# Gate column sums, late sums and output scaling placed elsewhere in a hybrid trunk layer

## The chip, the cores and the metric

One Trainium2 chip; the kernel runs on one core. The time is the device time of one launch in microseconds (us), of which three runs give the median. The engines are TensorE (PE; its weight loads are PEld), VectorE (DVE), ScalarE (ACT), GpSimd (POOL) and SyncE (SP); transfers between HBM and the on-chip memory are started from the queues of SP and POOL.

## What is computed

One layer of a decoder trunk in float32, with 512 positions, width 2048, and two branches that are merged by gates:

```python
mod = c_act @ w_ada[l] + b_ada[l]
shift, scale, gate = jnp.split(mod, 3, axis=-1)
h = rms_norm(x, g_pre[l]) * (1.0 + scale[:, None, :]) + shift[:, None, :]
p = h @ w_in[l]
cv, cg, cz, q, k, v, az, m_conv, m_attn = jnp.split(p, offsets, axis=-1)
y_conv = conv_branch(cv, cg, cz, ...)        # GLU, causal depthwise conv, layer norm, silu, silu(cz), projection
y_attn = attn_branch(q, k, v, az, ...)       # differential attention, rms norm, silu(az), projection
merged = jax.nn.sigmoid(m_conv) * y_conv + jax.nn.sigmoid(m_attn) * y_attn
out = merged @ w_o[l]
x = x + gate[:, None, :] * rms_norm(out, g_post[l])
```

The vector `gate` is the last third of `mod`: 2048 column sums of `c_act` times a 2048 x 2048 part of `w_ada`.

## The kernel before

**Matmuls.** A float32 product is emulated: `split` writes a value as a high part (a cast on ACT, line 145) and a low part (a subtraction on DVE, line 146), and `mm3` (line 167) makes three matmuls of them. So every weight tile that PE uses, `wh_...` and `wl_...`, comes through ACT and then DVE. Weights are fetched by SP (`wr_...`, up to 1 MB each, three buffers).

**Stages.** After the front, the first projections and the attention heads (0 to about 600 us) come, in this order: the last groups of the az projection (`gemm2`, tiles `pg_az`), three stages of `gemm_blocks` called cz (4 blocks), ma (8) and mc (8), the two branch projections ya and yc (`gemm_y`, tiles `py_ya`, `py_yc`, eight groups each), and the output projection by `w_o` in two column halves G=0 and G=1 (`oprod`, tiles `oz`, `or`, `ox`, `oy`). `gemm_blocks` makes a 2x2 block product with seven products z, x, y instead of eight; each needs a weight operand that is a sum of blocks (`ws_...`, DVE), split again. The output projection does the same, and for it the merged activations get block sums (`mt1`, `mt23`, `mt4`) while yc runs.

**Background work.** A deque `work` holds Python generators. `pump(n)` takes n steps from the first one, and is called between groups of matmuls: after each product of `gemm_blocks` (`rate[0]`, 1 there), after each group of ya (YP = 3) and of yc (3). `pump()` without a number runs all that is left. The block sums of `h` for cz (`block_sums`) are such a generator, and so is `gate(n)`, n = 0 to 3, for 512 columns of `gate` each: 16 steps, in each of which POOL starts the load of a 256 KB tile `adag` two steps ahead and DVE adds one tile times a scalar to `accg` (line 668); then one matmul with a matrix of ones, `pgt`, sums over the partitions and hands the result to every row; then `bg` and `gg` (lines 673 and 674). gate(1) is the first of the work in the az stage, gate(0) runs in mc stretched by `spread` to one step for every three products, gate(2) in ya, gate(3) in yc.

**Order.** The instructions of an engine run in the order that the tile scheduler gives them, which follows the program order, the dependencies and the free buffers; `paced` and `ordered` pin chains of them. A waiting instruction holds up all that stands behind it on its engine.

**End of yc, and the output.** The groups of yc go j = 0, 4, 1, 5, 2, 6, 3, 7; for each DVE merges two tiles `ga` (fetched by SP, lines 959 and 960), and for j >= 4 makes `mt23` and `mt4` (lines 972 to 974). Their splits are put into a list `late` and done during the first products of G=0 (`late_splits`). In G=1 the last `a22`, `a12` operands are prepared ahead (`held`), the rows of blocks 2 and 3 are scaled by `rstd` on ACT and added to x by accumulating DMAs of POOL (`xr2`, line 1209), and stored by SP (line 1212); blocks 0 and 1 follow (`finish`, line 1072).

## Time and profile before

| what | us |
|---|---|
| median of 3 runs | 1445.31 |
| lowest and highest | 1442.08, 1445.92 |
| the profiled execution, whole run | 1444.37 |
| its span (first to last instruction) | 1442.6 |
| PE busy in the span | 1383.1 |
| DVE busy in the span | 1159.9 |
| ACT busy in the span | 561.7 |

Times in the rows below count from the start of the span. The profiled execution is 1.8 us longer than its span. "Busy" is the time in which an engine worked on at least one instruction; for each instruction group the views give what ended the idle time before it. PEclk is the granted TensorE clock as a share of full speed.

### The profile page before, as it was taken

What the parts mean: (1) busy time and instruction counts of PE and PEld (TensorE: products, weight loads), DVE (VectorE), ACT (ScalarE), POOL (GpSimd) and SP (SyncE); (2) the same over time, 40 slices, a digit from 0 to 9 for tenths busy, and PEclk for the clock granted to TensorE, in tenths of its full rate; (3) what the DMA queues carried; (4) which work ended last, traced back from release to release, by engine and by line L of the source; (5) the groups of instructions that cost most, each with busy time, mean ns of one, the idle gap of its engine ahead of it and who ended that gap; (6) DMA issues with size and microseconds to landing.
All of it is one profiled execution on the core that took longest, in us unless ns stands there. A gap on an engine that the chain in (4) does not pass through costs nothing.

```text
span 1442.6 us, 20701 instructions
## 1 busy us (share of the span) xinstructions
PE 1383.1 (96%) x7903; PEld 1173.2 (81%) x7903; DVE 1159.9 (80%) x1882; ACT 561.7 (39%) x907; POOL 59.8 (4%) x103
## 2 busy tenths in 40 slices
...
GB/s 310 280 276 304 235 121 117 117 102 67 109 67 95 102 67 109 197 111 131 197 154 188 177 169 190 232 157 164 135 217 347 290 146 190 204 117 199 177 236 263
DMA packets 178758, 254.90 MB, mean 177 GB/s; under 512 B 10065, under 2 KB 120994, under 8 KB 178274
## 3 DMA queue, kind: packets, MB, share of 16 engines
...
## 4 chain that ended last, share of the span: by engine, by line
PE 78%; DVE 12%; DMA 5%; issue 3%; ACT 2%; SPq 0%; DVEq 0%; POOL 0%; ACTq 0%; POOLq 0%
PE pc L167 10%; PE py_ya L167 6%; PE pv L167 6%; PE pg_k L167 6%; PE pg_q L167 5%; PE x_ma L167 4%; PE x_mc L167 4%; PE pg_az L167 4%; PE y_mc L167 3%; PE y_ma L167 3%; PE z_ma L167 3%; PE z_mc L167 3%; PE x_cz L167 3%; PE oy L167 2%; PE or L167 2%
## 5 line engine op out<-in xcount | busy, mean ns | idle before, releaser
L500 DVE SCALAR_TENSOR_TENSOR cacc<-u,cw,cacc 128x511 f32<-128x511 f32 (+14 forms) x240 | 164.5, 729 | 0.0
L167 PE MATMUL pc<-hp,wh_c 128*128 128x512 f32 x512 | 159.8, 397 | 3.3 <-DVE part L369 1.2
L167 PEld LDWEIGHTS pc<-hp,wh_c 128*128 128x128 f32 x512 | 95.4, 189 | 29.3 <-issue 2.7
L167 PE MATMUL pc<-hp,wl_c 128*128 128x512 f32 x256 | 98.7, 395 | 2.1 <-DVE wl_c L146 2.1
L369 DVE TENSOR_TENSOR part<-pc,part 128x512 f32<-128x512 f32 x96 | 64.7, 688 | 25.4 <-PE pc L167 24.9
L167 PE MATMUL pv<-wh_v,hp 128*128 128x512 f32 x256 | 82.8, 397 | 0.9 <-DVE part L369 0.9
L167 PE MATMUL pg_q<-hp,wh_q 128*128 128x512 f32 x256 | 82.7, 399 | 0.0
L167 PE MATMUL pg_az<-hp,wh_az 128*128 128x512 f32 x256 | 82.1, 400 | 0.0
L167 PE MATMUL pg_k<-hp,wh_k 128*128 128x512 f32 x256 | 80.1, 392 | 0.0
L167 PE MATMUL py_ya<-ya,wh_ya 128*128 128x512 f32 x256 | 78.9, 389 | 0.0
L145 ACT CAST wh_c<-wr_c 128x1024 fp32r<-128x1024 f32 (+1 forms) x36 | 34.2, 956 | 104.6 <-PE pc L167 46.1
L167 PEld LDWEIGHTS pc<-hp,wl_c 128*128 128x128 f32 x256 | 48.4, 190 | 14.1 <-DVE wl_c L146 3.3
L167 PEld LDWEIGHTS pv<-wh_v,hp 128*128 128x128 f32 x256 | 47.8, 188 | 14.3 <-issue 4.5
L167 PEld LDWEIGHTS pg_az<-hp,wh_az 128*128 128x128 f32 x256 | 48.6, 191 | 12.3 <-issue 2.7
L652 POOL DMA_DIRECT2D adag<-in_w_ada_dram x64 | 34.4, 538 | 560.5 <-ACT ta_ma L753 277.8
L167 PEld LDWEIGHTS pg_q<-hp,wh_q 128*128 128x128 f32 x256 | 47.2, 188 | 12.4 <-issue 2.8
L167 PEld LDWEIGHTS py_ya<-ya,wh_ya 128*128 128x128 f32 x256 | 48.0, 188 | 9.9
L167 PEld LDWEIGHTS pg_k<-hp,wh_k 128*128 128x128 f32 x256 | 47.9, 188 | 9.4
L167 PE MATMUL pg_az<-hp,wl_az 128*128 128x512 f32 x128 | 50.8, 402 | 2.4 <-DVE wl_az L146 2.4
L167 PE MATMUL py_yc<-ych,wh_yc 128*128 128x512 f32 x128 | 50.8, 397 | 1.2 <-DVE ga L959 1.2
L307 DVE SCALAR_TENSOR_TENSOR acc<-ada,cact,acc 128x512 f32<-128x512 f32 (+1 forms) x52 | 50.5, 971 | 1.1 <-DMA ada<-in_w_ada_dram 0.9
L167 PE MATMUL py_yc<-ycl,wh_yc 128*128 128x512 f32 x128 | 51.1, 399 | 0.0
...
## 6 DMA issues: line engine op xcount, KB each, us to landing
ada<-in_w_ada_dram SPq DMA_DIRECT2D x128, 256.0 KB, 5.4
...
```

The lines of the kernel that those rows point to most:

```text
L145: nc.scalar.copy(hi, src)
L167: mm = nc.tensor.matmul(ps, a[p], b[q], start=start and i == 0, stop=stop and i == 2, skip_group_check=more)
L307: nc.vector.scalar_tensor_tensor(acc, raw[:, kk - k0, :, :], cact[:, kk:kk + 1], acc, op0=ALU.mult, op1=ALU.add)
L369: nc.vector.tensor_tensor(part[i], ps[f], part[i], op=ALU.add)
L500: paced(nc.vector.scalar_tensor_tensor(cvo[t][:, s:], u[t][:, :S - s], wj, cvo[t][:, s:], op0=ALU.mult, op1=ALU.add))
L652: nc.gpsimd.dma_start(out=raws[k], in_=ada_v[:, k, 2 * D + n * 512:2 * D + (n + 1) * 512])
```

## The change

It moves work and leaves the arithmetic as it was: gate(1) runs in mc behind gate(0) and `spread` is gone; each gate yields LAG = 5 more times ahead of its `pgt`; yc pumps four steps per group instead of three; in the last group of yc (j = 7) the sums `mt23`, `mt4` are put into `late` as well, and `late_steps` does four of its entries after the first products and two after each of the next; the last sum of G=0, `q + oy`, is placed inside the first step of G=1; in the tail the scaling and adding of row block 2 (`join(0)`) is placed between the preparation of the third and the fourth weight group.

```diff
@@ -667,6 +667,8 @@
             else:
                 nc.vector.scalar_tensor_tensor(acc, raws[k], s1, acc, op0=ALU.mult, op1=ALU.add)
             yield
+        for _ in range(LAG):
+            yield
         pgt = bank("t", 1, f"pgt_{n}")
         nc.tensor.matmul(pgt, ones, acc, start=True, stop=True)
         yield
@@ -678,13 +680,6 @@
             gg[0] = gp
         yield
 
-    def spread(steps, n):
-
-        for _ in steps:
-            for _ in range(n):
-                yield
-
-    work.append(gate(1))
     for pair in range(4):
         if pair == 1:
             work.append(block_sums())
@@ -851,7 +846,7 @@
             spill(f"cz{2 * pair + f}", gs[f])
     for c0, name in ((C_MA, "ma"), (C_MC, "mc")):
         if name == "mc":
-            work.append(spread(gate(0), 3))
+            work.extend((gate(0), gate(1)))
         for j in range(8):
             z, ta, tb = gemm_blocks(w_in[0], c0 + j * 256, f"{name}{j}")
             g0, g1 = temp(f"{name}0_{j}"), temp(f"{name}1_{j}")
@@ -933,10 +928,13 @@
     mB, mT1, mT23, mT4, late = [None] * KT, [None] * KH, [None] * KH, [None] * KH, []
     b12, t1 = {}, {}
 
-    def late_splits(n):
-        for _, g, hi, lo in late[:n]:
-            split(g, hi(), lo())
-        del late[:n]
+    def late_steps(n):
+        for _, step in sorted(late, key=lambda e: e[0])[:n]:
+            step()
+        late[:] = sorted(late, key=lambda e: e[0])[n:]
+
+    def late_split(order, g, hi, lo):
+        late.append((order, lambda: split(g, hi(), lo())))
 
     def late_page(box, i, name):
         def get():
@@ -968,22 +966,29 @@
                 split(u1, hi[:, H2:], lo[:, H2:])
                 continue
             split(g, hi, lo)
-            t23 = temp(f"mt23_{kk}")
-            nc.vector.tensor_tensor(t23[:, :H2], g[:, H2:], t1[j - 4][:, half], op=ALU.add)
-            nc.vector.tensor_tensor(t23[:, H2:], b12[kk][:, H2:], g[:, H2:], op=ALU.subtract)
-            nc.vector.tensor_tensor(t4[:, half], g[:, :H2], t23[:, :H2], op=ALU.subtract)
-            if kk < 4:
-                hi, lo = mT23[kk] = page(f"mt23h_{kk}", F32R), page(f"mt23l_{kk}", F32R)
-                split(t23, hi, lo)
+
+            def sums(kk=kk, half=half, g=g, u1=t1[j - 4][:, half], t4=t4, now=j < 7):
+                t23 = temp(f"mt23_{kk}")
+                nc.vector.tensor_tensor(t23[:, :H2], g[:, H2:], u1, op=ALU.add)
+                nc.vector.tensor_tensor(t23[:, H2:], b12[kk][:, H2:], g[:, H2:], op=ALU.subtract)
+                nc.vector.tensor_tensor(t4[:, half], g[:, :H2], t23[:, :H2], op=ALU.subtract)
+                if kk < 4:
+                    hi, lo = mT23[kk] = page(f"mt23h_{kk}", F32R), page(f"mt23l_{kk}", F32R)
+                    split(t23, hi, lo)
+                else:
+                    mT23[kk] = [None, None]
+                    late_split(kk if now else 8 + kk, t23, late_page(mT23[kk], 0, f"mt23h_{kk}"),
+                               late_page(mT23[kk], 1, f"mt23l_{kk}"))
+
+            if j < 7:
+                sums()
             else:
-                mT23[kk] = [None, None]
-                late.append((0, t23, late_page(mT23[kk], 0, f"mt23h_{kk}"), late_page(mT23[kk], 1, f"mt23l_{kk}")))
+                late.append((kk, sums))
         if j >= 4:
             mT4[j - 4] = [None, None]
-            late.append((1, t4, late_page(mT4[j - 4], 0, f"mt4h_{j}"), late_page(mT4[j - 4], 1, f"mt4l_{j}")))
-        pump(3)
+            late_split(16 + j, t4, late_page(mT4[j - 4], 0, f"mt4h_{j}"), late_page(mT4[j - 4], 1, f"mt4l_{j}"))
+        pump(4)
     pump()
-    late.sort(key=lambda e: e[0])
 
 
     fss = small(16, "fss")
@@ -1128,12 +1133,16 @@
                 p1()
                 paced(nc.vector.tensor_tensor(s1, a21, s1, op=ALU.add))
                 p7()
+                if G and t == 0:
+                    for i in range(2):
+                        nc.vector.tensor_tensor(u2[i], oy[i], u2[i], op=ALU.add)
+                        out_later(0, 2 + i, u2[i], u2[i], temp(f"osq12_0_{i}"))
                 p6()
                 p5()
             if t == 0:
                 out_now()
             if G == 0:
-                late_splits(2)
+                late_steps((4, 2, 2, 2)[t])
         if G:
 
             og01 = [pair_of(f"og01_{i}", F32) for i in range(2)]
@@ -1161,9 +1170,7 @@
                         nc.vector.tensor_tensor(g, orr[i], q[i], op=ALU.subtract)
                         out_later(1, i, g, g, temp(f"osq21_{G}_{i}"))
                 oprod(oy, wop_of(s2[2 * t:2 * t + 2], f"os4_{G}_{t}"), oB22, t, False)
-            for i in range(2):
-                nc.vector.tensor_tensor(q[i], oy[i], q[i], op=ALU.add)
-                out_later(0, 2 + i, q[i], q[i], temp(f"osq12_{G}_{i}"))
+            u2 = q
             continue
 
         oprod(oz, w12, oB21, 0, False)
@@ -1181,32 +1188,40 @@
                 og[t][n] = page(f"ogf_{n}_{t}")
                 fetch(f"og_{n}_{t}", og[t][n])
         held = []
-        for t in range(4):
+
+        def columns(t):
             rb = wraw(w_o[0], KH + 2 * t, 2, c0, 1024, f"ob_{G}_{t}") if t else rb0
-            a12, a22 = rb[:, :, :S], rb[:, :, S:]
-            if t < 2:
-                oprod(orr, wop(a22, f"oa22_{G}_{t}"), oT4, t, False)
-                if t:
-                    oprod(oz, wop(a12, f"oa12_{G}_{t}"), oB21, t, False)
-            else:
-                held.append((t, [wop_of([a[:, k, :] for k in range(2)], f"{n}_{t}", t == 2)
-                                 for a, n in ((a22, "oa22"), (a12, "oa12"))]))
-            if t == 1:
-                for i in range(2):
-                    g = temp(f"oc12_{i}")
-                    nc.vector.tensor_tensor(g, oy[i], q[i], op=ALU.add)
-                    out_done(2, 2 + i, g, og23[i][:, 0, :], page(f"osq12_{G}_{i}"))
-                sums3(2, 2)
-                r = rstd(2, 2)
+            return rb[:, :, :S], rb[:, :, S:]
+
+        def hold(t):
+            a12, a22 = columns(t)
+            held.append((t, [wop_of([a[:, k, :] for k in range(2)], f"{n}_{t}", t == 2)
+                             for a, n in ((a22, "oa22"), (a12, "oa12"))]))
+
+        def join(i):
+            for a, g in enumerate((og01[i], og23[i])):
+                nc.scalar.mul(g, g, r[:, i:i + 1])
+                nc.gpsimd.dma_start(out=xr2[i][a], in_=g, accum_op=ALU.add)
+
+        oprod(orr, wop(columns(0)[1], f"oa22_{G}_0"), oT4, 0, False)
+        a12, a22 = columns(1)
+        oprod(orr, wop(a22, f"oa22_{G}_1"), oT4, 1, False)
+        oprod(oz, wop(a12, f"oa12_{G}_1"), oB21, 1, False)
+        for i in range(2):
+            g = temp(f"oc12_{i}")
+            nc.vector.tensor_tensor(g, oy[i], q[i], op=ALU.add)
+            out_done(2, 2 + i, g, og23[i][:, 0, :], page(f"osq12_{G}_{i}"))
+        sums3(2, 2)
+        r = rstd(2, 2)
+        hold(2)
+        join(0)
+        hold(3)
+        join(1)
         xrs = []
         for i in range(2):
             xr = wp.tile([P, 4, 512], F32, tag="wr", name=f"xr_{i}")
             nc.sync.dma_start(out=xr.rearrange("p k n -> p (k n)"), in_=x2[i * P:(i + 1) * P, :])
             xrs.append(xr)
-        for i in range(2):
-            for a, g in enumerate((og01[i], og23[i])):
-                nc.scalar.mul(g, g, r[:, i:i + 1])
-                nc.gpsimd.dma_start(out=xr2[i][a], in_=g, accum_op=ALU.add)
         for i in range(2):
             for a in range(2):
                 nc.sync.dma_start(out=out2[(2 + i) * P:(3 + i) * P, a * 1024:(a + 1) * 1024],
```

How the scheduler's order changes, on DVE. First the az stage: the rows up to the split `wl_az2_0`, on which the third of the four az groups (`pg_az2`) waits. Names end in running numbers; `accg_1` and `adag_1_k` are gate(1), `hf`, `t1`, `t4`, `t23l` the block sums of `h`, `sz` the silu of an az group. Before:

```order
L668 SCALAR_TENSOR_TENSOR accg_1_5000<-adag_1_12_5089,cact_111,accg_1_5000 128x512
L621 TENSOR_TENSOR hf1_0_5241<-hp_0_341 128x512
L668 SCALAR_TENSOR_TENSOR accg_1_5000<-adag_1_13_5092,cact_111,accg_1_5000 128x512
L621 TENSOR_TENSOR hf2_0_5242<-hp_8_1387 128x512
L668 SCALAR_TENSOR_TENSOR accg_1_5000<-adag_1_14_5137,cact_111,accg_1_5000 128x512
L627 TENSOR_TENSOR t1_0_4942<-hf1_0_5241 128x256
L668 SCALAR_TENSOR_TENSOR accg_1_5000<-adag_1_15_5144,cact_111,accg_1_5000 128x512
L628 TENSOR_TENSOR hf1_0_5241<-hf1_0_5241,hf2_0_5242 128x256
L702 SCALAR_TENSOR_TENSOR sz_2_5272<-sz_2_5272,pg_az1_0_5129 128x512
L702 SCALAR_TENSOR_TENSOR sz_3_5277<-sz_3_5277,pg_az1_1_5130 128x512
L673 TENSOR_TENSOR bg_1_5139<-pgt_1_5177,bg_1_5139 128x512
L146 TENSOR_TENSOR wl_az2_0_5287<-wr_az2_0_5284,wh_az2_0_5286 128x1024
```

In the changed kernel:

```order
L621 TENSOR_TENSOR hf1_1_5167<-hp_1_515 128x512
L621 TENSOR_TENSOR hf2_1_5168<-hp_9_1392 128x512
L627 TENSOR_TENSOR t1_0_4942<-hf1_1_5167 128x256
L628 TENSOR_TENSOR hf1_1_5167<-hf1_1_5167,hf2_1_5168 128x256
L146 TENSOR_TENSOR wl_az1_12_5198<-wr_az1_8_5155,wh_az1_12_5197 128x1024
L630 TENSOR_TENSOR hf1_1_5167<-hf2_1_5168,t1_0_4942 128x256
L631 TENSOR_TENSOR t4_0_5128<-hf2_1_5168,hf1_1_5167 128x256
L146 TENSOR_TENSOR t23l_1_5204<-hf1_1_5167,t23h_1_5203 128x512
L146 TENSOR_TENSOR t4l_1_5208<-t4_0_5128,t4h_1_5207 128x512
L621 TENSOR_TENSOR hf1_2_5211<-hp_2_723 128x512
L621 TENSOR_TENSOR hf2_2_5212<-hp_10_1397 128x512
L146 TENSOR_TENSOR wl_az2_0_5255<-wr_az2_0_5252,wh_az2_0_5254 128x1024
```

The column sums and `bg_1` are gone from this stage; the block sums stand there now, further on by one `k` and a half than before when the same split comes. In mc, gate(0) and gate(1) stand with one `accg` per product.

Second the yc stage, around the last two column sums of gate(3) and the tiles `ga_4` and `ga_5` of the group j = 2. Before:

```order
L146 TENSOR_TENSOR wl_yc3_4_11780<-wr_yc3_11749,wh_yc3_4_11779 128x1024
L146 TENSOR_TENSOR mgs_4_11630<-mt1_2_11625,mgs_4_11630 128x256
L959 SCALAR_TENSOR_TENSOR ga_5_11636<-ga_5_11636,py_yc2_1_11566 128x512
L668 SCALAR_TENSOR_TENSOR accg_3_11265<-adag_3_14_11646,cact_111,accg_3_11265 128x512
L960 TENSOR_TENSOR ga_5_11636<-mg_4_10719,ga_5_11636 128x512
L966 TENSOR_TENSOR mt1_2_11625<-ga_5_11636 128x256
L668 SCALAR_TENSOR_TENSOR accg_3_11265<-adag_3_15_11653,cact_111,accg_3_11265 128x512
L146 TENSOR_TENSOR mgs_5_11640<-ga_5_11636,mgs_5_11640 128x256
```

In the changed kernel:

```order
L146 TENSOR_TENSOR wl_yc3_0_11752<-wr_yc3_11749,wh_yc3_0_11751 128x1024
L668 SCALAR_TENSOR_TENSOR accg_3_11265<-adag_3_14_11565,cact_111,accg_3_11265 128x512
L668 SCALAR_TENSOR_TENSOR accg_3_11265<-adag_3_15_11572,cact_111,accg_3_11265 128x512
L957 SCALAR_TENSOR_TENSOR ga_4_11638<-ga_4_11638,py_yc2_0_11577 128x512
L958 TENSOR_TENSOR ga_4_11638<-mg_4_10719,ga_4_11638 128x512
L964 TENSOR_TENSOR mt1_2_11637<-ga_4_11638 128x256
L146 TENSOR_TENSOR wl_yc3_4_11780<-wr_yc3_11749,wh_yc3_4_11779 128x1024
L146 TENSOR_TENSOR mgs_4_11642<-ga_4_11638,mgs_4_11642 128x256
L146 TENSOR_TENSOR mgs_4_11642<-mt1_2_11637,mgs_4_11642 128x256
L957 SCALAR_TENSOR_TENSOR ga_5_11648<-ga_5_11648,py_yc2_1_11578 128x512
```

`accg` 14 and 15 stood behind `ga_5` and stand ahead of `ga_4` now. On SP's queue the loads `wr_yc3` and `wr_yc7` stand ahead of two `ga` fetches each (`ga_2`, `ga_3` and `ga_10`, `ga_11`), which were ahead of them, and two fetches of `gg` ahead of `ga_4`.

Third the end of yc, up to the splits `wl_os2` for the first `ox` products of the output projection. Before:

```order
L146 TENSOR_TENSOR mt23l_6_12092<-mt23_6_11896,mt23h_6_12091 128x512
L959 SCALAR_TENSOR_TENSOR ga_15_11900<-ga_15_11900,py_yc7_1_11829 128x512
L960 TENSOR_TENSOR ga_15_11900<-mg_14_11104,ga_15_11900 128x512
L972 TENSOR_TENSOR mt23_7_11907<-ga_15_11900,mt1_3_11807 128x256
L973 TENSOR_TENSOR mt23_7_11907<-ga_7_11818,ga_15_11900 128x256
L146 TENSOR_TENSOR mgs_15_11904<-ga_15_11900,mgs_15_11904 128x512
L974 TENSOR_TENSOR mt4_7_11888<-ga_15_11900,mt23_7_11907 128x256
L1104 TENSOR_TENSOR os2_0_0_11981<-os1_0_0_11929,wr_oa_0_0_11927 128x512
L1104 TENSOR_TENSOR os2_0_1_11983<-os1_0_0_11929,wr_oa_0_0_11927 128x512
L146 TENSOR_TENSOR mt23l_7_12096<-mt23_7_11907,mt23h_7_12095 128x512
L146 TENSOR_TENSOR wl_os2_0_0_11986<-os2_0_0_11981,wh_os2_0_0_11985 128x512
L146 TENSOR_TENSOR wl_os2_0_0_11986<-os2_0_1_11983,wh_os2_0_0_11985 128x512
```

In the changed kernel:

```order
L146 TENSOR_TENSOR mgs_14_11893<-ga_14_11889,mgs_14_11893 128x512
L958 TENSOR_TENSOR ga_15_11896<-mg_14_11104,ga_15_11896 128x512
L146 TENSOR_TENSOR wl_os3_0_0_11958<-wr_oa_0_0_11919,wh_os3_0_0_11957 128x1024
L146 TENSOR_TENSOR mgs_15_11900<-ga_15_11896,mgs_15_11900 128x512
L1109 TENSOR_TENSOR os2_0_0_11973<-os1_0_0_11921,wr_oa_0_0_11919 128x512
L1109 TENSOR_TENSOR os2_0_1_11975<-os1_0_0_11921,wr_oa_0_0_11919 128x512
L972 TENSOR_TENSOR mt23_6_12005<-ga_14_11889,mt1_3_11807 128x256
L146 TENSOR_TENSOR wl_os2_0_0_11978<-os2_0_0_11973,wh_os2_0_0_11977 128x512
L973 TENSOR_TENSOR mt23_6_12005<-ga_6_11808,ga_14_11889 128x256
L974 TENSOR_TENSOR mt4_7_11888<-ga_14_11889,mt23_6_12005 128x256
L972 TENSOR_TENSOR mt23_7_12009<-ga_15_11896,mt1_3_11807 128x256
L146 TENSOR_TENSOR wl_os2_0_0_11978<-os2_0_1_11975,wh_os2_0_0_11977 128x512
```

Most sums of the last group (`mt23`, `mt4`) stood ahead of the sums `os2` and the splits `wl_os2`; all but one of those ahead of the first split stand behind it now, as do `mt23l_6` and `mt23l_7`.

## Rows read from the trace of the kernel before

**Rows 1.** The page, busy us, share of the span, instructions.
```profile
PE 1383.1 (96%) x7903; PEld 1173.2 (81%) x7903; DVE 1159.9 (80%) x1882; ACT 561.7 (39%) x907; POOL 59.8 (4%) x103
```

**Rows 2.** Waits of PE: waiting tile, line, releaser, us in all, times, longest.
```profile
PE pgt L671 <- DVE accg L668: 5.2, 2, 4.6
...
PE pg_az L167 <- DVE wl_az L146: 2.4, 2, 2.1
PE or L167 <- DVE wl_os L146: 2.2, 3, 0.8
...
PE x_cz L167 <- ACT wh_cz_s L145: 1.6, 1, 1.6
...
PE ox L167 <- ACT wh_os L145: 1.4, 1, 1.4
PE or L167 <- ACT wh_os L145: 1.4, 2, 0.7
...
PE py_yc L167 <- DVE ga L959: 1.2, 1, 1.2
...
PE x_cz L167 <- DVE wl_cz_s L146: 0.8, 1, 0.8
...
PE ox L167 <- DVE wl_os L146: 0.6, 1, 0.6
```

**Rows 3.** Windows: us, busy PE, PEld, DVE, ACT, POOL, PEclk, DMA share, GB/s.
```profile
626.00:629.00 3.00, 3.00 (x9) 2.32 (x8) 2.74 (x6) 0.43 (x1) 0.28 (x1) 0.50 0.23 87
677.00:680.00 3.00, 3.00 (x17) 3.00 (x17) 2.95 (x3) 0.18 (x1) 0.00 (x0) 0.53 0.04 10
1244.00:1247.00 3.00, 3.00 (x7) 2.02 (x7) 2.15 (x5) 0.62 (x1) 0.00 (x0) 0.50 0.17 59
```

**Rows 4.** Timeline of yc: start, us, engine, line, operation [idle before].
```profile
1232.46 0.54 POOL L652 DMA_DIRECT2D adag<-in_w_ada_dram  x1
...
1239.61 0.69 DVE L959 SCALAR_TENSOR_TENSOR ga<-ga,py_yc 128x512 f32<-128x512 f32 x1 [0.52 <-DMA ga<-scratch_mc]
1240.21 0.75 DVE L668 SCALAR_TENSOR_TENSOR accg<-adag,cact,accg 128x512 f32<-128x512 f32 x1
1240.88 0.68 DVE L960 TENSOR_TENSOR ga<-mg,ga 128x512 f32<-128x512 f32 x1
...
1241.94 0.75 DVE L668 SCALAR_TENSOR_TENSOR accg<-adag,cact,accg 128x512 f32<-128x512 f32 x1
...
1242.74 2.08 PE L671 MATMUL pgt<-accg,ones 128*128 128x512 f32 x2 [4.57 <-DVE accg L668]
```

**Rows 5.** Timeline of DVE, az and the start of cz.
```profile
605.39 8.63 DVE L668 SCALAR_TENSOR_TENSOR accg<-adag,cact,accg 128x512 f32<-128x512 f32 x11
...
623.62 1.21 DVE L146 TENSOR_TENSOR wl_az<-wr_az,wh_az 128x1024 fp32r<-128x1024 f32 x1
...
672.97 1.22 DVE L751 TENSOR_TENSOR ws_cz<-ws_cz,wr_cz 128x1024 f32<-128x1024 f32 x1
674.11 1.22 DVE L760 TENSOR_TENSOR wr_cz<-wr_cz 128x1024 f32<-128x1024 f32 x1
675.32 2.36 DVE L146 TENSOR_TENSOR wl_cz_s<-ws_cz,wh_cz_s 128x1024 fp32r<-128x1024 f32 x2
```

**Rows 6.** The tile adag, whole span: ns min/median/max; issue to landing.
```profile
L668 DVE SCALAR_TENSOR_TENSOR accg<-adag,cact,accg x60: 740/747/755, 605.4 to 1241.9; 128x512 f32<-128x512 f32 x60
...
DMA to landing us min/median/max: 2.9/4.3/8.2
```

**Rows 7.** Windows of 36 us in cz and mc, columns as in rows 3.
```profile
684.00:720.00 36.00, 36.00 (x302) 36.00 (x302) 34.58 (x45) 19.50 (x27) 0.00 (x0) 1.00 0.59 197
936.00:972.00 36.00, 36.00 (x302) 36.00 (x302) 30.05 (x35) 15.63 (x20) 2.69 (x5) 1.00 0.52 165
```

**Rows 8.** Timeline of DVE, start of G=1.
```profile
1348.21 1.28 DVE L1165 TENSOR_TENSOR oq<-oy,oq 128x512 f32<-128x512 f32 x2
```

**Rows 9.** Window in the tail, columns as in rows 3.
```profile
1420.00:1425.00 5.00, 5.00 (x24) 4.14 (x23) 3.27 (x13) 2.74 (x6) 2.28 (x3) 1.00 0.98 309
```

## The prediction

> **What bounds it now.** The page first: TensorE (PE) is busy 1383.1 of 1442.6 us, 96% [rows 1]. A gain can only be idle PE time or PE time at half clock; work taken off VectorE (DVE), the queues or ScalarE counts where PE stands still for it. So the second view is what PE waits for [rows 2]. Leaving out the front and the heads, which the change does not touch, it names nine kinds: the gate's bank read `pgt` behind its column sums (5.2 us in two places, the longest 4.6), `pg_az` behind a DVE weight split (2.4), the first cz products (1.6 and 0.8), one `py_yc` (1.2), and the first `ox` and the `or` products of the output projection (1.4, 0.6, 1.4, 2.2). Third, the granted clock right behind three of these waits [rows 3]: 0.50 from 626 to 629 us, 0.53 from 677 to 680 and 0.50 from 1244 to 1247, so the level of 1.2 GHz instead of 2.4. PE does half its work there: 1.5 us lost in the first, 1.4 in the second; in the third PE runs from 1242.7 [rows 4] to at least 1247, 4.3 us, and loses 2.1.
>
> **Part 1, gate(1) leaves the az stage.** Its sums held DVE from 605.39, eleven in 8.63 us, and five more stand before or among the block sums; the weight split for `pg_az` came only at 623.62 [rows 5], behind `pgt` and `bg`, hence PE's 0.6 and 2.1 us. In the new order no row of a gate stands there; between the last head's `on` and `wl_az2_0` stand 21 rows of block sums, `sz` and weight splits, where before it were 26, 17 of them the gate's. DVE gives back 16 sums of 0.75 [rows 6], 12 us, and the two operations behind `pgt`. Laid out with 1.14 us from start to start of a 128x1024 (672.97 to 674.11 [rows 5]) and 0.67 of a 128x512 (1240.21 to 1240.88 [rows 4]), I find `wl_az2_0` at 616 against a need at 620, and the only split near its need is `wl_az2_4`, at most 0.3 late. Gain 0.6 + 2.1 + 1.5 - 0.3 = **3.9**, from 0.3 (the same long wait and its clock one group later) to 4.2.
>
> The same 12 us are what cz's first block lacked: DVE came to the second of its weight sums only at 672.97, and to the split behind them at 675.32 [rows 5], while PE waited 1.6 for the cast and then 0.8 for the split [rows 2]. With the block sums done earlier that split is due some 5 us before PE wants it, so an error of 2 us in my layout changes nothing. Gain 1.6 + 0.8 + 1.4 = **3.8**, from 1 (the clock falls again) to 3.8.
>
> **Part 2, where that work goes.** Both gates(0 and 1) now run in mc, one step per product instead of one in three, 46 steps in 56 products of 2.86 us. Does DVE still keep up? A block is 7 products, 20.0 us of PE. DVE must issue eleven 128x1024 (1.14), five 128x256 (0.34, the half of 0.67) and now seven `accg` (0.67): 12.5 + 1.7 + 4.7 = 18.9 of 20.0. By full durations, 1.22 and 0.75 in [rows 4, 5] and 0.4, it would be 20.7, 0.7 over, or 5.6 in eight blocks. The nearest row decides for the first: in cz the same block with its own fillers keeps DVE at 34.58 of 36.00 us and PE does not wait at all, where mc now has 30.05 [rows 7]. PE gets two `pgt` of 1.1 us in either place, no change. Then the loads: each step issues a 256 KB load two steps (5.7 us) ahead, and loads landed in 2.9 to 8.2 us, median 4.3 [rows 6]. Most are in time; a few late ones eat DVE's 1.1 us of slack in a block and then PE. I take **-1.0**, from 0 to -5.6. The queued work behind a late `accg` is the next weight split, on which PE's next product waits.
>
> Here a rule speaks against the change. The Trainium skill, "SBUF — State Buffer", section "SBUF: two separate sides", says that a DMA issued from GpSimd has its descriptors written by the GpSimd cores, and that a VectorE instruction in a two-port mode locks these out, so that such a DMA starves while VectorE is busy. All `adag` loads go that way, and they move to the stage that fills DVE most. The rows speak mildly against it, since the median of 4.3 us is over all stages; whether DVE's instructions here run in that mode no row shows. By the rule this part would cost rival A's price, by the row 1.0.
>
> **Part 3, gate(3) in yc.** PE stood 4.6 us at `pgt` until `accg` 15, started at 1241.94 [rows 4]. Two things were late: the load of `adag` 15, issued by POOL only at 1232.46, and the DVE queue, which sat on `ga` (another fetch) until 1239.61 [rows 4]. With four steps per group of products the loads are issued one group earlier (10.9 us a group, 48 matmuls; my layout has the last at 1224.6, landed by 1231), and the order shows sums 14 and 15 ahead of `ga_4`, that is ahead of the late fetches. `pgt` keeps its place on PE (need 1237.4 if nothing slips; sums done by 1232 to 1234). The old loss is 4.6 + 2.1 + 1.2 = 7.9. New risk: on SP's queue the 1 MB weight loads of yc3 and yc7 now stand ahead of two `ga` fetches each, and DVE serves `ga` in order, with the next weight split behind it. The row at 1239.61 shows DVE standing 0.52 for such a fetch, and the one `py_yc` wait of 1.2 [rows 2] is behind another. I put 0.75 us of PE wait, between these, at two groups, and for the bound twice the 1.2 and its half clock of 1.5 on top. Gain **6.4**, from 7.9 - 2 x 2.7 = 2.5 to 7.9.
>
> **Part 4, late sums of the last group.** Before the first `os2` split DVE now has five 128x256 sums and two 128x512 splits less: 5 x 0.34 + 2 x 0.67 = 3.0 us. `ox` waited 1.4 + 0.6 = 2.0; that goes. But the sums still run before the next weights, only the two splits (1.3) move behind, and PE arrives 2.0 earlier, so the next `or`, whose split has as many rows ahead of it as before, waits 0.7 more. Gain **1.3**, from 0 to 2.0.
>
> **Part 5, q + oy of the first half joins the second half.** It held DVE for 1.28 at 1348.21, just ahead of the sum whose split PE waited for [rows 8]. In the new order the second of the two `oq` stands behind that sum, and sum, cast and split come half of the 1.28 sooner; `or` waited 0.6 + 0.8 there, more than that. Gain **0.6**, from 0 to 0.6.
>
> **Part 6, join(0) between hold(2) and hold(3).** ScalarE scales row block 2 some 2.6 us earlier, so the accumulating transfers of that block start about that much earlier, and the stores at the end wait for them. But the DMA share is 0.98 from 1420 on [rows 9]: the tail is bytes, and only what the earlier start moves ahead of 1420 is saved. Against that the casts of hold(3) come one scaling later, and PE may wait 0.3 to 0.5. Gain **0.7**, from -0.5 to 2.
>
> **The sum.** 3.9 + 3.8 - 1.0 + 6.4 + 1.3 + 0.6 + 0.7 = 15.7. The profiled execution took 1444.37; it lies 0.9 under the median of 1445.31 and inside the spread of 1442.08 to 1445.92, so it stands for the kernel, and 1444.4 - 15.7 = **1428.7**. With every part at its high end the gain is 4.2 + 3.8 + 7.9 + 2.0 + 0.6 + 2 = 20.5 and the time 1424; with every part at its low end it is 0.3 + 1 - 5.6 + 2.5 - 0.5 = -2.3, no change, which needs six mishaps.
>
> **Rivals.**
> A. *mc becomes DMA-bound on POOL's loads, and the kernel slower.* DVE is in order, so a late `adag` stops PE. A load may take 5.7 us unseen, and slack per product is 1.1/7 = 0.2. The 32 loads eat the 16.7 us gained elsewhere when each costs PE 0.5, that is from a mean landing of 6.4 us; at 7.0 they cost 32 x 1.1 = 35, and it is 1463. For: 8.2 has occurred [rows 6], and each load waits for a free temp buffer first. Against: the median 4.3, and that `accg` waited for no load in the list of DVE waits.
> B. *One late load per block only.* 8.2 - 5.7 - 0.2 = 2.3 at most for one, half of it on average, 8 x 1.15 = 9 instead of 1.0: 1437.
> C. *yc's wait changes its name.* The `ga` fetches, behind 1 MB loads, stop DVE and the `py_yc` products wait as in part 3's bound: gain 2.5 instead of 6.4, 1433.
> D. *az waits one group later.* A split that loses its place behind the block sums costs 2.1 + 1.5 again: 1432.
> E. *The change does not do what it says.* DVE has the same 1880 rows in both orders; where it runs full, work taken from one wait comes back at the next. With B, C and D together the gain is 15.7 - 8 - 3.9 - 3.6 = 0.2: 1444.
>
> **How the numbers follow.** Chances: forecast 0.62 (own range 1422 to 1433), C 0.12, D 0.06, B 0.07, E 0.07, A 0.06. The range 1421 to 1440 leaves out E and A, 0.13; its low end is the high ends' 1424 and 3 us, by which runs of one kernel differ. A measurement of this kernel tells 0.3%, 4.3 us, from no change; faster by more is forecast, B, C and D, 0.87; same is E, 0.07; slower is A, 0.06.
>
> **What would show it.** In the waits of PE, `pg_az` on `wl_az`, `x_cz` on `wh_cz_s` and `pgt` on `accg` gone or under 0.5 us, and the three half-clock stretches with them; PE at 36.00 of 36 us through mc with DVE near 34; `oz` starting 6 to 7 us sooner after the first ya product than now; `ox` without a wait, `or` with some 0.8 more. I am wrong if PE waits for `x_mc` many times (A, B), if `py_yc` waits on `ga` for over 3 us (C), or if a half-clock stretch stays where no wait is left.

## The result, and the profile after

The changed kernel takes **1427.79 us** (median of 4 runs, 1426.52 to 1429.52) where the kernel before takes 1444.46 (median of 4 runs, 1442.08 to 1445.92): a ratio of 0.9887, interval 0.9869 to 0.9905, so 16.7 us faster. Forecast were 1428.7, between 1421 and 1440, with a chance of 0.87 for faster. A second round, run e9 below, gave 1427.82 and 0.9903 (0.9884 to 0.9921). The total was right, and most of its terms were. Three of the reasons were not, and one term had the wrong size.

The page of the changed kernel, part 1, answers to [rows 1]:

```profile
span 1426.1 us, 20678 instructions
PE 1379.1 (97%) x7903; PEld 1171.8 (82%) x7903; DVE 1158.4 (81%) x1882; ACT 560.9 (39%) x907; POOL 59.6 (4%) x103
```

PE lost 4.0 us of busy time though it runs the same 7903 matmuls: that is mostly time at half clock given back (the mean granted clock over the span is 0.990 before and 0.994 after). The other 12.5 of the span's 16.5 are idle PE time. What PE waits for, after the heads, answers to [rows 2]:

```profile
PE or L167 <- DVE wl_os L146: 2.8, 4, 0.8
...
PE or L167 <- ACT wh_os L145: 1.2, 1, 1.2
...
PE oz L167 <- DVE ga L957: 1.2, 1, 1.2
...
PE or L167 <- DVE wl_oa L146: 0.3, 1, 0.3
PE py_yc L167 <- DVE ga L957: 0.3, 1, 0.3
```

Gone are `pgt`, `pg_az`, both `x_cz` waits and both `ox` waits. New are one `oz` wait of 1.2 on `ga` and 0.6 more of `or` on `wl_os`. The windows (columns as in [rows 3]) at two of the times where the clock had fallen, and two that answer to [rows 7]:

```profile
626.00:629.00 3.00, 3.00 (x14) 2.19 (x13) 2.93 (x6) 1.45 (x2) 0.00 (x0) 1.00 0.08 14
677.00:680.00 3.00, 3.00 (x27) 3.00 (x26) 3.00 (x5) 1.65 (x2) 0.00 (x0) 1.00 0.38 85
936.00:972.00 36.00, 36.00 (x302) 36.00 (x301) 32.43 (x38) 15.93 (x19) 2.13 (x4) 1.00 0.53 172
972.00:1008.00 36.00, 36.00 (x297) 35.52 (x296) 32.69 (x41) 15.17 (x20) 7.49 (x14) 1.00 0.76 236
```

The granted clock is 1.00 in all of them. The stages begin up to 18 us earlier than before, so these are not the same places of the program; but cut into 3 us windows, the trace shows no granted clock under 0.97 from 540 to 1410 us, where the kernel before has three such stretches. In mc PE works 36.00 of 36 us with DVE at 32.4 to 32.7 instead of 30.05. The sum by stage is worked out from the starts of the stages' first matmuls in both traces. The last column is from PE's last matmul to the end of the span.

| us | front | az | cz | ma | mc | ya | yc | output | end |
|---|---|---|---|---|---|---|---|---|---|
| before | 558.50 | 111.33 | 86.76 | 163.39 | 163.09 | 87.53 | 96.81 | 160.31 | 14.88 |
| changed | 559.62 | 105.19 | 82.37 | 162.76 | 163.39 | 87.53 | 88.98 | 161.29 | 14.99 |
| changed, e9 | 557.96 | 105.19 | 82.37 | 162.77 | 163.39 | 87.53 | 88.40 | 159.42 | 14.87 |

So az gave 6.1, cz 4.4, ma 0.6 (its one wait of 0.4, `x_ma` on `tb_ma`, is gone) and yc 7.8; mc took 0.3, the output 1.0, the end 0.1, and the front, which the change does not touch, 1.1. From 1427.9 and 1423.7, the profiled executions of one and the same kernel, one sees what such a table can tell: az to ya repeat within 0.01 us, while the front differs by 1.7 and the output by 1.9, where the expectation of e9 had less than 0.7 for every stage behind the front. Nor do the others always repeat: mc is 163.39 or 163.40 in e1, e3, e10 and e11 too, but 164.53 in e12 with no edit there. In e2, e4, e5 and e6, whose mc is that of the kernel before, it is 163.82 to 164.19 instead of 163.09, and in e4 to e6 yc, unchanged as well, is 95.09 to 96.37 instead of 96.81.

### The profile page after: what moved, and what is told of

It is laid out like the page before. It is cut to its first block, busy times and chain, and to the rows that moved or that the text cites. A ratio compares the mean times of both kernels' runs of the same rounds, so it can differ in the third digit from the quotient of the medians.

```text
span 1426.1 us, 20678 instructions
## 1 busy us (share of the span) xinstructions
PE 1379.1 (97%) x7903; PEld 1171.8 (82%) x7903; DVE 1158.4 (81%) x1882; ACT 560.9 (39%) x907; POOL 59.6 (4%) x103
## 4 chain that ended last, share of the span: by engine, by line
PE 81%; DVE 10%; DMA 4%; issue 2%; ACT 2%; SPq 1%; DVEq 0%; ACTq 0%
PE pc L167 11%; PE py_ya L167 6%; PE pv L167 6%; PE pg_k L167 6%; PE pg_az L167 5%; PE pg_q L167 5%; PE x_ma L167 5%; PE x_mc L167 5%; PE z_mc L167 3%; PE z_ma L167 3%; PE y_ma L167 3%; PE y_mc L167 3%; PE x_cz L167 2%; PE oy L167 2%; DMA ga<-scratch_mc 2%
## 5 line engine op out<-in xcount | busy, mean ns | idle before, releaser
L167 PEld LDWEIGHTS pc<-hp,wh_c 128*128 128x128 f32 x512 | 95.9, 190 | 29.1 <-issue 2.7
L167 PEld LDWEIGHTS pc<-hp,wl_c 128*128 128x128 f32 x256 | 48.5, 190 | 14.1 <-DVE wl_c L146 3.3
L167 PE MATMUL pg_k<-hp,wl_k 128*128 128x512 f32 x128 | 51.1, 399 | 0.0
L167 PE MATMUL pv<-wl_v,hp 128*128 128x512 f32 x128 | 50.6, 396 | 0.0
```

What stands on the lines that cost most here:

```text
L167: mm = nc.tensor.matmul(ps, a[p], b[q], start=start and i == 0, stop=stop and i == 2, skip_group_check=more)
```

## The experiments

The theory was that of the prediction: DVE's time for the gate is what az and cz lacked, mc has room for it, and yc's wait was late loads and late `ga` fetches. The rivals: order alone counts, not DVE's time; mc's loads come late; the yc wait changes its name. Each expectation was written before its run. Stage times below are worked out as in the table; times with a ratio are medians of 4 runs or more, the others single runs.

### One part of the change alone: gates and LAG (e1), four steps in yc (e2), no late sums (e3)

e1 is the kernel before with gate(0), gate(1) in mc and the LAG, yc still at three steps; e2 is the kernel before with four steps; e3 the changed kernel with the old late splits.

```diff
# e1, against before (spread and its call are gone)
+        for _ in range(LAG):
+            yield
-    work.append(gate(1))
-            work.append(spread(gate(0), 3))
+            work.extend((gate(0), gate(1)))
# e2, against before
-        pump(3)
+        pump(4)
# e3, against changed
-                late.append((kk, sums))
# and in its place the sums at once, as before
-                late_steps((4, 2, 2, 2)[t])
+                late_splits(2)
```

> The kernel before with gate(0) and gate(1) in mc, one step per product, and with the LAG yields ahead of every pgt; yc still pumps three steps, the late sums and the tail are as before. Theory (DVE time of the column sums held up the weight splits): first pg_az to first z_cz 105.2 us instead of 111.3, cz 82.4 instead of 86.8, mc within 0.5 of before, no pg_az, x_cz or x_mc wait over 0.4 us. In yc, LAG alone puts pgt_3 at the end of the last group on PE, while its last loads and sums stay as late as before; if only the place of pgt on PE matters the 4.6 us wait is gone here too and yc takes 90 to 91 us, time 1427 to 1430; if the earlier loads of pump(4) are what matters (as the prediction said) it stays, yc takes 96 to 97, time 1434 to 1436.

> The kernel before with pump(4) in yc as its one edit: sums 14 and 15 come ahead of ga_4, but without LAG pgt_3 stands 28 matmuls earlier on PE than before. Theory (loads and sums issued earlier are what matters): the pgt wait falls from 4.6 to under 1.5 us, yc takes 90 to 92 us instead of 96.8, time about 1439. Rival (it is the distance between the last sum and pgt, which LAG gives): the wait stays at 3 us or more, yc 94 to 97, time 1442 to 1444. az and cz as before, 111 and 87.

> The changed kernel with the old handling of the late splits (the sums of j = 7 made in yc, two splits after each product). Theory (part 4 of the prediction): ox waits about 2 us again and the first 26 matmul groups of the output projection take 1 to 2.5 us longer, time 1429 to 1430. Rival (the start of the output projection is bound by how late the last ga tiles land, whatever the order of the sums): the waits only change names, start of the output projection within 0.5, time 1427 to 1428.5. All else as in the changed kernel.

| run | us | ratio to before | az | cz | mc | yc | output |
|---|---|---|---|---|---|---|---|
| e1 | 1428.1 (1426.92 to 1430.77) | 0.9896 (0.9871 to 0.9921) | 105.20 | 82.37 | 163.40 | 89.39 | 163.87 |
| e2 | 1438.46 (1434.93 to 1441.87) | 0.9971 (0.9954 to 0.9989) | 111.32 | 86.76 | 163.83 | 90.33 | 161.65 |
| e3 | 1427.41 (1424.96 to 1429.26) | 0.9884 (0.9861 to 0.9907) | 105.18 | 82.37 | 163.39 | 88.70 | 162.88 |

e1 has most of the gain, 14.1 us in its round, and its interval overlaps that of the changed kernel; the parts that it lacks are too small for the times to tell. In the trace they show as an output stage of 163.87 instead of 161.29 and 159.42. In yc either edit alone brings most of the 7.8: 7.4 and 6.5. PE's waits in yc, of e1 and then of e2:

```profile
PE py_yc L167 <- DVE ga L954: 1.1, 1, 1.1
```

```profile
PE pgt L671 <- DVE accg L668: 1.0, 1, 1.0
```

In e1 the last sum starts at 1225.97 and `pgt` stands at the end of the stage, at 1245.6, so it waits for nothing. In e2 the last sum starts at 1231.90, and `pgt`, 28 matmuls earlier than before in PE's order, starts at 1232.71 after a wait of 1.0. Counted from the first matmul of yc, the last sum starts after 71.3 us before, 69.3 in e1, 60.0 in e2 and 60.3 in the changed kernel, and `pgt` stands behind 289, 384, 261 and 288 matmuls of yc. The 4.6 of [rows 2] was therefore the distance between the last sum and `pgt`; the earlier load is one way to lengthen it, the LAG another.

The median of e3 is 0.7 us from that of e1 and 0.4 from that of the changed kernel, well within their spread; the 1429 to 1430 of its expectation did not come. Its trace has the `ox` wait of [rows 2] back to the digit. PE's waits from 1240 to 1275:

```profile
PE ox L167 <- ACT wh_os L145: 1.4, 1, 1.4
...
PE oz L167 <- DVE ga L954: 0.9, 1, 0.9
...
PE ox L167 <- DVE wl_os L146: 0.6, 1, 0.6
```

The two `or` products that follow waited 0.75 and 0.75 before. In the changed kernel and in e9 `ox` does not wait, but these two wait 1.2 and 0.8 and an earlier `or` 0.6 or 0.15: net 1.0 and 1.4 us gained. In e1 and e2, which have the old late sums, these waits were followed by half clock besides (0.54 from 1267 to 1270 in e1), in e3 and in the kernel before they were not. What hides all this in the times is the start of the output itself: from the first `oz` to its third group it took 26.5 us before, 27.4 and 25.5 in two executions of the changed kernel, 29.1 in e3 and 30.1 in e1. It holds these waits, those on `ga` (below) and the half clock behind them.

### Is it DVE's time, or DVE's order? (e4, e5, e6)

Three kernels made from the one before; gate(1) stays in az. In e4 its sums cover one column instead of 512, so 511 of 512 columns of `gate` in that quarter are left out. In e5 the az stage pumps five steps instead of three. In e6 the block sums stand ahead of gate(1).

```diff
# e4: n == 1, k >= 1
-                nc.vector.scalar_tensor_tensor(acc, raws[k], s1, acc, op0=ALU.mult, op1=ALU.add)
+                nc.vector.scalar_tensor_tensor(acc[:, :1], raws[k][:, :1], s1, acc[:, :1], op0=ALU.mult, op1=ALU.add)
# e5
-PUMP2 = 3
+PUMP2 = 5
# e6
+    work.append(block_sums())
     work.append(gate(1))
...
-            work.append(block_sums())
```

> The kernel before, with gate(1) where it was, all its loads, instructions, its pgt and its order, but its column sums over one column instead of 512 (the other 511 columns of this part of the gate are left out). Theory (DVE time): the 2.1 us pg_az wait and the x_cz waits go, az (first pg_az to first z_cz) takes 106 to 107 us (the pgt of 1.1 is still in it), cz 82 to 83. Rival (the 20 transfers of POOL, or where pgt stands on PE): az stays at 110 to 111, cz at 86 to 87.

> The kernel before with PUMP2 = 5 instead of 3, so that the block sums of h are taken from the deque faster in the az stage; gate(1) stays in front of them with all its sums, loads and its pgt. In DVE's order the first cz weight sums (ws_cz) now stand ahead of the last sz, which waits for the last az product on PE; before they stand behind it. The prediction's theory for cz (the 12 us of DVE time of gate(1) are what cz's first block lacked): the time is still spent in az, so the x_cz waits of 1.6 and 0.8 us stay, cz 86 to 87. The rival that the run with thin sums suggests (it is the place of ws_cz behind the last sz): the x_cz waits go, cz 82 to 83, az 110 to 114.

> The kernel before with block_sums put into the deque ahead of gate(1) from the start of az, so that the block sums are done early and gate(1) runs at the end of az; ws_cz stays behind the last sz in DVE's order, with bg between. Rival of the prediction (place of ws_cz): the x_cz waits stay at 2 us or more in all, cz 85 to 88, and more if bg's wait for pgt comes on top. Prediction's theory (DVE time): the 12 us still lie in az and cz, which says the same for cz; for az it says 108 to 112.

| | us | az | cz |
|---|---|---|---|
| before (profiled) | 1444.37 | 111.33 | 86.76 |
| e4 thin sums | 1439.36 | 108.45 | 85.26 |
| e5 faster pump | 1452.34 | 124.76 | 82.37 |
| e6 block sums first | 1456.75 | 121.59 | 90.22 |
| changed | 1427.9 | 105.19 | 82.37 |

PE's waits of e4 from 590 to 700, and then DVE's timeline there around the start of cz:

```profile
PE x_cz L167 <- ACT wh_cz_s L145: 1.6, 1, 1.6
PE pg_az L167 <- DVE wl_az L146: 1.4, 2, 1.1
PE x_cz L167 <- DVE wl_cz_s L146: 0.8, 1, 0.8
```

```profile
666.96 1.28 DVE L704 SCALAR_TENSOR_TENSOR sz<-sz,pg_az 128x512 f32<-128x512 f32 x2
668.15 1.22 DVE L752 TENSOR_TENSOR ws_cz<-wr_cz,wr_cz 128x1024 f32<-128x1024 f32 x1
```

In az, less DVE time does help: the `pgt` wait is gone, `pg_az` waits 1.4 instead of 2.4, no half-clock stretch follows, and az is 2.9 shorter (108.45, where 106 to 107 was expected). In cz it does nothing: 1.6 and 0.8, the very numbers of [rows 2], although DVE has some 8 of the gate's 12 us less to do ahead (eleven sums in 2.78 us, where [rows 5] has 8.63). (Cz, at 85.26 between the two expectations, is 1.5 shorter only because the clock stays at 1.00 behind those waits.) The two DVE rows say why. The weight sum `ws_cz` stands right behind the last `sz`, which reads the last `pg_az` product from PE through ScalarE. In the kernel before it is the same pair, 3.6 us later. DVE is not idle just ahead of it: in both kernels it works without a gap for 21.4 us, from the `sz` of the group before to those of the last one, at block sums and weight splits. But it had stood for an earlier `sz`, and there e4 lost again most of what it had saved: 7.92 us where the kernel before stood 2.09. The rows are of e4, DVE and ScalarE:

```profile
615.40 0.69 DVE L704 SCALAR_TENSOR_TENSOR sz<-sz,pg_az 128x512 f32<-128x512 f32 x1 [7.92 <-ACT sz L703]
...
645.51 0.69 DVE L704 SCALAR_TENSOR_TENSOR sz<-sz,pg_az 128x512 f32<-128x512 f32 x1 [0.15 <-ACT sz L703]
```

```profile
666.22 1.08 ACT L703 ACTIVATE sz<-pg_az 128x512 f32<-128x512 f32 x2
```

The first of the two ScalarE instructions, 0.59 long, ends at 666.81, and DVE's `sz` starts at 666.96. So even a DVE with nothing to do ahead of it would have come to `ws_cz` only some 0.15 to 0.3 us sooner (an estimate from these rows): with this order it cannot start until PE has ended az, and PE then waits for what follows it. The changed kernel's DVE timeline has the other order:

```profile
659.04 1.22 DVE L745 TENSOR_TENSOR ws_cz<-wr_cz,wr_cz 128x1024 f32<-128x1024 f32 x1
...
662.76 1.23 DVE L146 TENSOR_TENSOR wl_cz_s<-ws_cz,wh_cz_s 128x1024 fp32r<-128x1024 f32 x1
...
665.16 0.68 DVE L697 SCALAR_TENSOR_TENSOR sz<-sz,pg_az 128x512 f32<-128x512 f32 x1
```

e5 has gate(1) in az as before but drains the block sums early enough that `ws_cz` comes ahead of the last `sz`; its cz is 82.37, to the digit that of the changed kernel, while its az pays for it, 13.4 us where the expectation had up to 3. The longest waits of PE in az and cz of e5, and then its wait at the start of cz in e6 with two rows of DVE:

```profile
PE pg_az L167 <- DVE wl_az L146: 8.8, 5, 4.1
PE pgt L671 <- DVE accg L668: 3.5, 1, 3.5
```

```profile
PE x_cz L167 <- ACT wh_cz_s L145: 4.4, 1, 4.4
```

```profile
678.78 1.37 DVE L702 SCALAR_TENSOR_TENSOR sz<-sz,pg_az 128x512 f32<-128x512 f32 x2 [2.10 <-ACT sz L701]
...
684.15 1.23 DVE L750 TENSOR_TENSOR ws_cz<-wr_cz,wr_cz 128x1024 f32<-128x1024 f32 x1 [2.67 <-DMA scratch_gg<-gg]
```

In e6 the gate is what is left at the end of az, the `x_cz` wait grows to 4.4, and cz to 90.22 (az to 121.59, where up to 112 was expected). Here DVE does stand idle ahead of the last `sz`, 2.1 us, and `ws_cz` still comes late: behind that `sz`, behind `bg` and `gg` of the gate, and 2.67 us behind the store of `gg`, by the second row. So what decides cz is the place of `ws_cz`, and not how much time DVE has ahead of it; both order and time decide az.

### How much room mc has (e7, e8)

e7 issues the loads of `adag` one step ahead instead of two. e8 adds to each column sum of gates 0 and 1 but the first a second one, times 0.0, of the same size: 30 sums, some 20 us of DVE (30 times 0.67).

```diff
# e7, against changed
-        load(1)
-            load(k + 2)
+            load(k + 1)
# e8, against changed
+            if n < 2 and k:
+                nc.vector.scalar_tensor_tensor(acc, raws[k], 0.0, acc, op0=ALU.mult, op1=ALU.add)
```

> The changed kernel with each gate's load written one step ahead instead of two. The prediction (a load may take the two steps, 5.7 us, unseen): with one step, 2.9 us, against a landing of 4.5, some 32 steps of mc are 1.4 us late each, mc 200 us or more instead of 163.4, and yc gets its pgt wait back in part. Rival (POOL runs ahead of the steps and is held by free buffers alone): mc 163 to 165, yc within 1 us of 89.0, landing as before.

> The changed kernel with one more full column sum (times zero) behind each of the 30 sums k >= 1 of gate(0) and gate(1), so DVE has 20 us more to do in mc. Theory (DVE has a slack of some 1.1 to 2 us a block there and is the next bound): mc 173 to 178 us instead of 163.4, with x_mc and z_mc, y_mc waits on weight splits. Rival 1 (DVE was already full, the 18.9 of 20.0 is the limit): mc 183. Rival 2 (DVE is far from the limit): mc under 167.

e7 took 1434.4, with mc 167.93 (4.5 more than changed) and yc 94.23; e8 took 1440.1, with mc 173.45 (10.1 more). PE's waits of e7, 900 to 1250; those of e8, 900 to 1080; and a window of e8:

```profile
PE py_yc L167 <- DVE ga L956: 4.1, 1, 4.1
PE x_mc L167 <- DVE tb_mc L757: 2.8, 1, 2.8
```

```profile
PE y_mc L167 <- DVE wl_mc_s L146: 3.4, 2, 2.8
PE x_mc L167 <- DVE wl_mc_s L146: 1.9, 1, 1.9
```

```profile
936.00:972.00 36.00, 33.10 (x256) 32.22 (x255) 35.26 (x46) 13.54 (x16) 3.73 (x7) 0.95 0.56 182
```

Neither expectation for e7 came: mc is not 200 us, and not 163 to 165 either. The one wait in mc, 2.8 us, with a half-clock stretch behind it (0.56 from 927 to 930), is not of an `adag` load. DVE stood there for a weight load of SP:

```profile
924.93 1.22 DVE L744 TENSOR_TENSOR ws_mc<-wr_mc,wr_mc 128x1024 f32<-128x1024 f32 x1 [3.67 <-DMA wr_mc<-in_w_in_dram]
```

No column sum waited for its load in e7, as none did in the kernel before and in the changed one. Taking the n-th issue and the n-th sum together, the loads of mc were issued 10.2 to 27.4 us ahead of their sums in e7, median 15.5, and 9.0 to 26.6, median 14.8, in the changed kernel. The prediction reckoned with 5.7, and with 2.9 for one step. So the lead is not counted in steps. The view of the tile `adag` for e7 names what POOL waits for ahead of its issues (us, times), and how long the loads take; the second fence has the changed kernel's:

```profile
  DVE accg L667: 68.8, 18
...
DMA to landing us min/median/max: 2.9/4.5/7.5
```

```profile
DMA to landing us min/median/max: 3.0/4.5/7.0
```

POOL waits for `accg`, that is for a buffer that a sum has read, and then issues. The wait of 4.1 in e7's yc, for a `ga` fetch, has half clock behind it too (0.55 from 1224 to 1227). Whether the edit made that fetch and the weight load late, no run shows: e7 is a single run, and in e12, with no edit in mc, DVE also stands up to 2.1 us for a `wr_mc`.

e8, a single run too, tells how much DVE can take: of 20 us some 10 were absorbed and 10 came out as waits and half clock.

### The new wait behind `ga`, and the end (e9 to e12)

e9 is the changed kernel again, as the measure for the other three. e12 is the changed kernel with the old tail (both `join` behind the last weights). e11 moves the three `gg` fetches from ahead of the output projection to behind the third step of G=0; e10 does that too, and writes the two `ga` fetches of a yc group ahead of its weight load.

```diff
# e10, against changed; e11 has the gg lines alone
+        gas = [temp(f"ga_{2 * j + f}") for f in range(2)]
+        for f in range(2):
+            fetch(f"mc{2 * j + f}", gas[f])
         py = gemm_y(w_conv_out[0], j * 256, yc, f"yc{j}")
...
-            g = temp(f"ga_{k}")
-            fetch(f"mc{k}", g)
+            g = gas[f]
...
-    for n in range(1, 4):
-        gg[n] = page(f"gg_{n}")
-        fetch(f"gg{n}", gg[n])
...
                 late_steps((4, 2, 2, 2)[t])
+                if t == 2:
+                    for n in range(1, 4):
+                        gg[n] = page(f"gg_{n}")
+                        fetch(f"gg{n}", gg[n])
```

> The changed kernel itself, timed beside the three others of this call: 1426 to 1430 us, as measured. Its stages show what differs between executions with no edit: the front up to the first az product may differ by some 4 us (555.4 to 559.9 in the executions so far), every later stage by less than 0.7.

> The changed kernel with the two ga fetches of each yc group written ahead of its weight load instead of behind its products, and the three gg fetches behind the third step of the output projection. In SP's order ga_6 and ga_7 then stand ahead of the load wr_oa_0_2, which waits for a free buffer. Theory (what is left at the start of the output projection is DVE behind a late ga fetch, 2.7 us at 1245): the oz wait of 1.2 us goes and yc with the first 26.5 us of the output projection takes 2 to 3 us less, time 1425 to 1426. Rival (DVE is full there in any case, ga or not): under 1 us, time as the changed kernel within 1.

> The changed kernel with only the three gg fetches moved behind the third step of the output projection; in SP's order ga_4 and ga_5 no longer stand behind two of them, and wr_oa_0_2 and ga_6 no longer behind gg_3, which waits for gate(3)'s spill. Theory (SP's queue, held by gg_3, made ga_6 late): the start of the output projection takes 1 to 2 us less. Rival (the buffer of wr_oa_0_2 holds the queue for as long): within 0.5 us of the changed kernel.

> The changed kernel with the old order of the tail (scaling and adding of rows 2 and 3 behind the preparation of all weight groups). The prediction (part 6): the last PE matmul to the end of the span takes 0.7 us longer, from -0.5 to 2. Rival, from the two traces (14.9 and 15.0 us with either order: the last accumulating transfer lands 4.8 and 5.1 us after PE's end, bytes bind): within 0.4 us, and the 0.3 us wait of or on wl_oa goes, so the old tail is no slower.

| run | us | ratio to before | yc | start of output | PE's end to span's end |
|---|---|---|---|---|---|
| e9 changed | 1427.82 (1423.67 to 1431.26) | 0.9903 (0.9884 to 0.9921) | 88.40 | 25.51 | 14.87 |
| e10 fetches first | 1424.46 (1420.64 to 1425.76) | 0.9868 (0.9849 to 0.9888) | 88.40 | 23.37 | 15.12 |
| e11 gg late | 1426.48 (1425.61 to 1430.39) | 0.9892 (0.9872 to 0.9911) | 89.40 | 27.83 | 15.04 |
| e12 old tail | 1428.45 (1427.59 to 1428.96) | 0.99 (0.9883 to 0.9916) | 90.19 | 28.31 | 15.04 |

"Start of output" is from the first `oz` to its third group. The wait in question, in the changed kernel's timeline: DVE stands 2.74 us for a fetch, and PE's `oz` stands for DVE a little later.

```profile
1245.15 0.69 DVE L957 SCALAR_TENSOR_TENSOR ga<-ga,py_yc 128x512 f32<-128x512 f32 x1 [2.74 <-DMA ga<-scratch_mc]
...
1251.82 0.50 PE L167 MATMUL oz<-wh_oa,mgs 128*128 128x512 f32 x1 [1.15 <-DVE ga L957]
```

SP's queue there shows the four fetches behind the third `gg` fetch, ahead of which the queue stood 9 us, and a 1 MB weight load. The second fence is the queue of e11, with no `gg` there: it stands 10.5 us ahead of the weight load itself.

```profile
1227.78 0.42 SPq L438 DMA_DIRECT2D ga<-scratch_mc  x1
1237.02 0.32 SPq L438 DMA_DIRECT2D gg<-scratch_gg  x1
1238.03 0.38 SPq L155 DMA_DIRECT2D wr_oa<-in_w_o_dram  x1
1238.46 2.10 SPq L438 DMA_DIRECT2D ga<-scratch_mc  x4
```

```profile
1225.50 0.42 SPq L438 DMA_DIRECT2D ga<-scratch_mc  x1
1236.46 0.38 SPq L155 DMA_DIRECT2D wr_oa<-in_w_o_dram  x1
```

In e10 two of the four fetches stand ahead of that load, and the list of DVE's waits from 1160 to 1275 changes from the changed kernel's first row to that of e10 in the second fence:

```profile
DVE ga L957 <- DMA ga<-scratch_mc: 9.6, 5, 2.7
```

```profile
DVE ga L959 <- PE py_yc L167: 7.9, 5, 2.7
```

DVE now waits for PE, which is the bound, and no longer for a fetch. The start of the output is the shortest of all, and the median is 3.4 us under that of e9 (its interval ends at 0.9888, just above where that of e9 begins, 0.9884, so the two are not wholly apart). It has the lowest median of all here. e11 leaves the fetches behind the weight load, and DVE still stands 9.3 us for them in five times. Yc and the start of the output together take 117.2 us in e11, 111.8 in e10, and 116.4, 113.9 and 118.5 in the changed kernel, e9 and e12, so moving `gg` alone gains nothing that can be told. The queue is held by `gg` in the one and by the weight load's buffer in the other, for about as long; in e10, with `gg` out of the way and two of the fetches ahead of the load, they come in time. The earlier fetches with `gg` in its old place were not run.

e12 differs from e9 by 0.6 us, inside both spreads: the tail edit is worth nothing that can be measured. From PE's end to the span's end it is 14.6 to 15.1 us in the seven traces with the new tail and 14.8 to 15.2 in the seven with the old one. POOL's accumulating transfers in the tail, in the changed kernel, where PE ends at 1411.12, and then in e12, where it ends at 1412.14:

```profile
1399.92 0.87 POOL L1204 DMA_DIRECT2D xr<-og  x1 [0.69 <-ACT og L1203]
1403.57 0.87 POOL L1204 DMA_DIRECT2D xr<-og  x1 [2.77 <-DVE wl_oa L146]
```

```profile
1404.09 0.87 POOL L1217 DMA_DIRECT2D xr<-og  x1 [3.29 <-PE or L167]
1405.13 0.87 POOL L1217 DMA_DIRECT2D xr<-og  x1 [0.17 <-DVE oc L1226]
```

The rows are the second and the third of four transfers. Counted back from PE's end, the second starts 11.2 us ahead instead of 8.1, but the third and the fourth, of the other row block, 7.6 and 6.5 instead of 7.0 and 6.0. What is stored last was hardly moved, and PE pays 0.3 for it (`or` on `wl_oa`).

## Why the prediction was right, and where its steps were not

**Part 1, az: right.** 3.9 forecast. Az shrank by 6.1, of which 1.1 is `pgt` of gate(1), which now runs in mc. The 5.0 left are the waits named (0.7 and 2.4 in a list of that stretch) and the clock; the forecast's 1.5 for the clock came from one 3 us window, and a stretch reaches past its edges (0.83 from 624 to 627). Rival D, the wait one group later, did not come: no `pg_az` wait is left.

**Part 1, cz: the gain right, the reason wrong.** The step "The same 12 us are what cz's first block lacked" failed. e4 took 8 of the 12 us of DVE's gate time away and the waits of 1.6 and 0.8 stayed; e5 left the gate in place and they went. The time saved was spent standing for an earlier `sz` (7.92 us in e4). The waits hung on `ws_cz` standing behind the last `sz`. Moving the gate away helped because the block sums then stand further ahead in the order and run out sooner, so that the scheduler puts `ws_cz` ahead of the last `sz`. The prediction's "with the block sums done earlier" was right; that DVE's time alone would do it was not. 4.4 against 3.8, by the clock's edges again.

**Part 2, mc: right in effect, too dear, and with a wrong clock for the loads.** Forecast -1.0, measured -0.3 with one `pgt` more (1.1) in the stage, so the sums themselves cost nothing; the mc of unchanged kernels varies by as much as 1.1. DVE's room was bigger than 1.1 us a block: 20 us more, in the first six of the eight blocks, cost only 10 (e8). "A load may take 5.7 us unseen" failed: the loads were issued a median of 14.8 us ahead, and e7, with half the written lead, has 15.5 and no sum that waits for a load. The loads are held by free buffers, not by steps.

**Rivals A and B** did not happen. `adag` landed in 3.0 to 7.0 us, median 4.5, against 2.9 to 8.2, median 4.3 [rows 6], with DVE at 90% of its time in mc. That bears on the rule of the Trainium skill, "SBUF — State Buffer", section "SBUF: two separate sides", by which a VectorE instruction in a two-port mode starves a DMA issued from GpSimd: this case's rows show no such starving beside these DVE instructions. Whether they run in the mode that the rule speaks of, no run here shows.

**Part 3, yc: right in size, half the reason.** Forecast 6.4, measured 7.8 and, in e9, 8.4. "The loads are issued one group earlier" is what pump(4) does, and "`pgt` keeps its place" is true of pump(4) and the LAG together (behind 288 matmuls instead of 289). But e1 shows that the LAG alone, which moves `pgt` and leaves the loads late, does nearly as much, and e2 that pump(4) alone, with `pgt` earlier, leaves a wait of 1.0. Rival C, the `ga` fetches stopping PE, was wrong by a place: `py_yc` waits only 0.3, but the wait turns up at `oz` with 1.2, or 2.0 in e12, or not at all (e9). The prediction priced this and put it into yc. A slip of the part on the change belongs here: of the fetches named there only `ga_2` and `ga_10` had stood ahead of `wr_yc3` and `wr_yc7`; `ga_3` and `ga_11` stood behind them already.

**Part 4, late sums: about right.** 1.3 forecast; `ox` lost its 2.0 and `or` took back 0.6 and 1.0 where 0.7 was foreseen: net 1.0 to 1.4 in the traces, and more where the clock would have fallen. The times of e3 and the changed kernel do not show it.

**Part 5, q + oy: right.** `or` at the start of G=1 waited 0.6 and 0.8; in e3, e9 and the changed kernel one wait of 0.8 is left there, in e1, with the old place, both are there. 0.6 as forecast.

**Part 6, join(0): the term was mis-sized.** 0.7 forecast, nothing measured: 14.99 and 14.87 from PE's end to the span's end, where it was 14.88, and PE pays 0.3. The step "only what the earlier start moves ahead of 1420 is saved" counted row block 2, but row block 3 is the last to be stored, and its transfers start only 0.5 sooner.

**The sum.** The forecast of 15.7 was 0.8 under the 16.5 between the two profiled executions. Az, cz, mc and yc gave 2.2 + 0.6 + 0.7 + 1.4 more than forecast, ma 0.6 unforeseen. The output came out 1.0 worse where parts 4 and 5 had 1.9 better, and the end 0.1 worse where part 6 had 0.7 better. The front took 1.1 by chance: its length lies between 555.4 and 560.6 in these executions whatever the kernel. That the total came within 0.9 of the measured time is in part luck: the better az and yc were cancelled by the output and the front.
